# Index scores of a streaming encoder: heads taken two at a time, both PSUM banks claimed, the two 64-row products issued one behind the other

## The chip, the cores and the metric

The kernel runs on one core of one Trainium2 chip. The metric is device time in microseconds (us) of one execution of the program; a lower time is better. Engines are named as the profile names them: PE is TensorE (PEld its weight loads), DVE is VectorE, ACT is ScalarE, POOL is GpSimd, and SP is SyncE, which here only issues DMAs. Each engine takes its own instructions strictly in the order in which they were written for it; an instruction that waits holds up all that stands behind it on that engine.

## The reference

One layer of an encoder is applied to 512 prompt rows and 64 sample rows, 1024 wide, in float32. What matters here is the sparse attention's indexer. Each row has 8 small index queries of 64 numbers and 8 head weights; each key has one index vector of 64 numbers:

```
dots  = einsum('bqhd,bld->bqhl', qi, ki_all) * (IDX_DIM ** -0.5)          # 8 heads, IDX_DIM = 64
score = einsum('bqh,bqhl->bql', wi * (N_IDX_HEADS ** -0.5), relu(dots))   # one number for a row and a key
score = where(admissible, score, NEG_INF)
_, idx = top_k(score, top_k)        # the keys that this row attends to
...                                 # softmax attention over them, 8 heads of 128
y = conv_branch(...)                # depthwise convolution of 31 taps, LayerNorm, swish, projection
mix = (g_att * (o @ w_att_out) + g_conv * y) @ w_o
...                                 # LayerNorm, then a mixture of 16 experts, then LayerNorm
```

The products with the big weights (`w_in`, `w_conv_out`, `w_att_out`, `w_o`) come before, between and after these steps.

## The kernel before

Rows are taken in five tiles: t = 0 to 3 are 128 prompt rows each, t = 4 is the 64 sample rows. A product with a big weight is done in three parts, since weight and input are both split into a rounded high part and the rest (`whi`, `wlo`; `hh`, `hl`). ACT casts `whi` (line 139), DVE subtracts to get `wlo` (line 140), and PE runs three passes for each piece (lines 242 to 244 in `fm_step`, where weights are stationary and 288 tokens stream, the output tile is `acc`; lines 144 to 146 with tokens stationary). `whi` and `wlo` have three buffers, so a cast waits until PE has read an old one.

`select(t)` computes the index scores of a tile and marks the best keys. For each of the 8 heads PE multiplies the head's queries with all keys of the tile's range (line 528): 128 columns of queries are stationary, L keys stream, L is 256, 384 and 512 for t = 1, 2, 3 and 192 for t = 4 (t = 0 needs no selection). The contracted length is only 64. Two heads share a slab of `qiT`: even heads lie in partitions 0 to 63 and odd heads in partitions 64 to 127, and `kiT` holds the keys twice, once in each half. Each float32 product becomes two instructions on PE. The result goes to a PSUM bank of the group `dot`, which has two banks:

```
    def dot(name="dot"):
        return psum.tile([128, 512], F32, name=name, tag="dot", bufs=2)
```

ACT takes it out with a Relu into `rl` (line 530, two buffers), and DVE weighs and adds it to `sc` (lines 532 and 534). DVE then finds the best keys in rounds of a maximum of eight and a replacement (lines 540 and 541) and turns `sc` into a bias. The attention's logits `pl` (line 652) use the same two `dot` banks; DVE reads them in `softmax` (line 639). ACT and PE follow with exponentials, transposes `pp` (line 656) and products `po` (line 660).

Around these steps stand, in program order, the query projections (`tm`, with `stq` taken out by ACT on line 570), the convolution of 8 channel blocks on DVE (line 588), its LayerNorm (lines 612 to 629), 16 gate logits (`gate_logits`, an `fm` product each, its tanh `glg` by ACT on line 709), the split of the convolution's output into `yh` and `yl` (lines 720 and 721), then the products with `w_conv_out` (line 735, inputs `yh`, `yl`) and `w_att_out` (line 741, inputs `oh`, `ol`). The instruction order on each engine is not the program's order: a scheduler with a model of the engines sorts all of it ahead of time, by priority and by when it believes operands to be ready. So the gate logits' and the convolution's `fm` products fill PE between the steps of selection and attention. In the experts' stage the order of PE, DVE and ACT is written by hand, and SP issues the weight loads `ring` (line 1083) behind reads of expert numbers into its registers (line 1308, `TENSOR_LOAD order`).

Of the kernel before, what the change touches and what calls it, by code (L numbers as in the profile page):

```python
# [14 lines left out]
AF = mybir.ActivationFunctionType  # L15
OP = mybir.AluOpType
# [42 lines left out]
def encoder_step(ctx: ExitStack, tc: tile.TileContext, a, o):  # L59
    nc = tc.nc  # L60
    V, S, G, PE, SY = nc.vector, nc.scalar, nc.gpsimd, nc.tensor, nc.sync
# [21 lines left out]
    def trp(name="trp"):  # L83
        return psum.tile([128, 512], F32, name=name, tag="trp", bufs=2)

    def dot(name="dot"):
        return psum.tile([128, 512], F32, name=name, tag="dot", bufs=2)
# [187 lines left out]
    def first_steps(ks):  # L275
        for i in range(3):
            for k in ks:
                for h in range(2):
                    st = fm_step(gps[i], gw3[i], h, k, hh, hl)
        return st  # L280
# [5 lines left out]
    for c in range(4):  # L286
# [4 lines left out]
        st = first_steps([2 * c])  # L291
# [38 lines left out]
    def fm(src, ncols, c0, xh, xl, m=128):  # L330
        with tc.high_priority(offset=400):
            raw = wcols(src, ncols, c0, m)
            ada_next("load")
            with tc.issue_after(hlast):
                w = split(raw, [128, KT, m])
        ps = [acc(), acc()]
        ada_next("product")
        for h in range(2):
            for k in range(KT):
                fm_step(ps, w, h, k, xh, xl, m)  # L340
        return ps
# [90 lines left out]
    qiT = at2[:, 0:2304].rearrange("p (h t) -> p h t", h=4)  # L432
    kiT = at2[:, 2304:3008]
# [18 lines left out]
    def tm(c0, n, kstep):  # L452
        ps = [(acc, acc, acc, dot, fifth)[t](f"tm{t}") for t in range(NT)]
        for k0 in range(0, KT, kstep):
            with tc.high_priority():
                raw = wload(dap(a["w_in"], k0 * 128 * NIN + c0, [[NIN, 128], [128 * NIN, kstep], [1, n]]),
                            [128, kstep, n])
                wh, wl = split(raw, [128, kstep, n])
            order = [(k, t) for k in range(k0, k0 + kstep) for t in range(NT)]
            if k0 + kstep == KT:  # L460
                order = [(k, t) for t in range(NT) for k in range(k0, KT)]
            tokens_product(ps, k0, kstep, hh, hl, hs, wh, wl)
        return ps
# [11 lines left out]
    def rope_heads(x, n, nh, rot, tab):  # L475
        rope(x.rearrange("p (h d) -> p h d", h=nh), rot,
             lambda c0, w: tab[0:n, None, c0:c0 + w].to_broadcast([n, nh, w]))


    def turn(dst, src, t):  # L480
        if t < 4:
            PE.transpose(dst, src, ident)
        else:
            PE.matmul(dst, src, ident2, start=True, stop=True)
# [4 lines left out]
    ps = fm(a["w_in"], NIN, C_KI, hh, hl, 72)  # L489
# [20 lines left out]
    ps = tm(C_QI, 512, 2)  # L510
    for t in range(NT):
        n = TS[t]
        st = misc.tile([128, 512], F32, name="st", tag=("S", "rl")[t % 2], bufs=2)
# [4 lines left out]
            turn(pk[:, 128 * i:128 * i + n], st[:, 128 * i:128 * i + 128], t)  # L518
        S.copy(qiT[:, :, 128 * t:128 * t + n], pk.rearrange("p (h t) -> p h t", h=4)[:, :, 0:n])

    def select(t):
        n, L, k0 = TS[t], (128 * (t + 1), 192)[t == 4], (0, SEQ)[t == 4]
        rounds = (KP, KS)[t == 4] // 8
        sc = misc.tile([128, L], F32, name=f"sc{t}", tag=f"sc{t}", bufs=1)
        for h in range(8):
            pr = slice(64 * (h % 2), 64 * (h % 2) + 64)
            pdt = dot("pdot")
            PE.matmul(pdt[0:n, 0:L], qiT[pr, h // 2, 128 * t:128 * t + n], kiT[pr, k0:k0 + L], start=True, stop=True)  # L528
            rl = misc.tile([128, 512], F32, name="rl", tag="rl", bufs=2)
            S.activation(rl[0:n, 0:L], pdt[0:n, 0:L], AF.Relu, scale=0.125)  # L530
            if h == 0:
                V.tensor_scalar(sc[0:n, 0:L], rl[0:n, 0:L], wis[0:n, t, 0:1], 0.0, op0=OP.mult, op1=OP.add)
            else:
                V.scalar_tensor_tensor(sc[0:n, 0:L], rl[0:n, 0:L], wis[0:n, t, h:h + 1], sc[0:n, 0:L],
                                       op0=OP.mult, op1=OP.add)
        if t < 4:
            V.memset(sc[0:64, L - 64:L], NEG)
        m8 = misc.tile([128, 8], F32, name="m8", tag="m8", bufs=2)
        for r in range(rounds):
            V.max(m8[0:n], sc[0:n, 0:L])  # L540
            V.match_replace(sc[0:n, 0:L], m8[0:n], sc[0:n, 0:L], MARK)
        V.tensor_scalar(sc[0:n, 0:L], sc[0:n, 0:L], MARK, NEG, op0=OP.not_equal, op1=OP.mult)
        return sc

    ps = tm(C_K, 512, 2)
    for t in range(NT):
        n = TS[t]
        st = misc.tile([128, 512], F32, name="stk", tag=("S", "rl")[t % 2], bufs=2)
# [16 lines left out]
    for c in range(2):  # L565
        ps = tm(C_Q + 512 * c, 512, 2)
        for t in range(NT):
            n = TS[t]
            st = misc.tile([128, 512], F32, name="stq", tag=("S", "rl")[t % 2], bufs=2)
            S.copy(st, ps[t])  # L570
            rope_heads(st, 128, 4, 32, rq[:, t, :])
            pk = trp("pq")
            for i in range(4):
                turn(pk[:, 128 * i:128 * i + n], st[:, 128 * i:128 * i + 128], t)
            S.copy(qT[:, 4 * c:4 * c + 4, 128 * t:128 * t + n], pk.rearrange("p (h t) -> p h t", h=4)[:, :, 0:n])
# [26 lines left out]
    bias = {0: bias0}  # L602
# [31 lines left out]
    SCL = HD ** -0.5  # L634

    def softmax(pl, bias, L):
        lg = misc.tile([128, 512], F32, name="lg", tag="lg", bufs=3)
        sm = misc.tile([128, 4], F32, name="sm", tag="sm", bufs=4)
        V.tensor_tensor_reduce(lg[:, 0:L], pl[:, 0:L], bias[:, 0:L], -SCL, 3e38, OP.add, OP.min, sm[:, 0:1])
        S.activation(lg[:, 0:L], lg[:, 0:L], AF.Exp, bias=sm[:, 0:1], scale=-1.0, accum_out=sm[:, 1:2])  # L640
        V.reciprocal(sm[:, 2:3], sm[:, 1:2])
        S.activation(lg[:, 0:L], lg[:, 0:L], AF.Copy, scale=sm[:, 2:3])
        return lg

    def att_prompt(t):
        L = 128 * (t + 1)
        for g in range(2):
            po = fifth("po")
            for hh_ in range(4):
                h = 4 * g + hh_  # L650
                pl = dot("pl")
                PE.matmul(pl[:, 0:L], qT[:, h, 128 * t:128 * t + 128], kT[:, g, 0:L], start=True, stop=True)  # L652
                lg = softmax(pl, bias[t], L)
                pp = trp("pp")
                for kb in range(t + 1):
                    PE.transpose(pp[:, 128 * kb:128 * kb + 128], lg[:, 128 * kb:128 * kb + 128], ident)
                pT = misc.tile([128, 512], F32, name="pT", tag="S", bufs=2)
                S.copy(pT[:, 0:L], pp[:, 0:L])
                for kb in range(t + 1):
                    PE.matmul(po[:, 128 * hh_:128 * hh_ + 128], vtm[:, kb, 128 * g:128 * g + 128],  # L660
                              pT[:, 128 * kb:128 * kb + 128], start=kb == 0, stop=kb == t)
            pov = po.rearrange("p (h t) -> p h t", h=4)
            dst = (slice(None), slice(4 * g, 4 * g + 4), slice(128 * t, 128 * t + 128))
            S.copy(oh[dst], pov)
            V.tensor_tensor(ol[dst], pov, oh[dst], op=OP.subtract)

    def att_sample():
        for g in range(2):
# [21 lines left out]
            V.tensor_tensor(ol[dst], pov, oh[dst], op=OP.subtract)  # L690

    bias[1] = select(1)
    bias[2] = select(2)
    att_prompt(0)
    conv_ln()
    bias[4] = select(4)
    twice = G.dma_start(bias[4][64:128, 0:192], bias[4][0:64, 0:192]).ins
    bias[3] = select(3)
# [150 lines left out]
    ps = [(acc, acc, acc, dot, fifth)[t](f"o{t}") for t in range(NT)]  # L849
# [117 lines left out]
    for t in range(NT):  # L967
        n = TS[t]
# [54 lines left out]
    for j in range(2):  # L1023
        V.tensor_tensor(Ej[:, j], Ej[:, j], bc(w12[:, :, j], 16), op=OP.mult)
        for t in range(NT):
            n = TS[t]
            PE.matmul(pwt[:, 0:16], ohr[0:n, j, t, :].bitcast(F32), Ej[0:n, j, t, :], start=t == 0 and j == 0,
                      stop=t == NT - 1 and j == 1)
# [337 lines left out]
    with tc.manual_schedule(engines={mybir.EngineType.PE, mybir.EngineType.DVE, mybir.EngineType.Activation}):  # L1366
# [15 lines left out]
        for u, x in enumerate(units):  # L1382
            if u == 2:
                for y in units:
                    i = y.es[0] - NFIX
# [126 lines left out]
    for t in range(NT):  # L1512
        n, s = TS[t], int(t == 4)
# [50 lines left out]
```

## Time and profile before

| what | us |
|---|---|
| three timed executions: lowest, median, highest | 869.45, 880.91, 880.99 |
| the profiled execution, its own time | 876.71 |
| its span, first to last instruction | 875.0 |
| PE busy in the span | 791.9 |
| DVE busy | 640.5 |
| ACT busy | 358.6 |
| all 64 instructions of the index products (line 528), first and last start | 278.4 and 394.8 |

The profile is that of one execution. Its span and the execution's own time differ by 1.7 us, which lie ahead of the first and behind the last instruction. The profile gives busy time per engine, the idle time ahead of each group of instructions and what ended it, the instructions in order of time, and the chain of waits: the work that ended last, followed backwards from the end. Matmuls overlap in the pipeline and their ends are modelled, so the distance between two starts says more of their price than the length of one.

### The profile page before, as it was taken

The page shows a single profiled execution, that of the slowest core. Times are in us where ns is not written, and L with a number is a line of the kernel's source. Part 1 is how long each engine was busy: PE and PEld are TensorE (multiplying, and loading weights), DVE is VectorE, ACT ScalarE, POOL GpSimd, SP SyncE. Part 2 cuts the span into 40 slices and gives each one's busy share as a digit, 9 for nine tenths or more (in the row PEclk, how much of TensorE's full clock was granted, in tenths as well). Part 3 has the DMA queues.
Part 4 walks back from the last instruction along what each step waited for, and adds up shares of the span by engine and source line. Part 5 has one row for each costly group of instructions (what it writes and reads, how often), then busy time and mean ns, then how long its engine had stood idle before and what let it go on. Part 6 is the DMA issues. An engine that isn't in the chain of part 4 may idle for free.

```text
span 875.0 us, 13257 instructions
## 1 busy us (share of the span) xinstructions
PE 791.9 (90%) x4827; PEld 640.9 (73%) x4827; DVE 640.5 (73%) x1255; ACT 358.6 (41%) x654; POOL 143.6 (16%) x172
## 2 busy tenths in 40 slices
PE   4899999999999999999999999799947999999920
PEld 3788888887878879879899789788836667645400
DVE  1569999989999889988896425437797697555516
ACT  3243232324344335547743852222433564344205
POOL 2300000310200000000100001020257532322220
PEclk9999999999999999999999999899956999999975
DMA  9997664491423224232443105677597999799525
GB/s 289 342 352 254 204 201 126 120 246 56 148 75 89 83 75 115 89 100 62 135 127 106 54 1 194 224 214 260 116 273 242 346 348 316 200 335 386 149 46 201
DMA packets 108866, 159.70 MB, mean 183 GB/s; under 512 B 9715, under 2 KB 67211, under 8 KB 108801
## 3 DMA queue, kind: packets, MB, share of 16 engines
q1 hardware_dynamic: 94464, 120.38, 42.1%
q0 software_dynamic: 12736, 34.26, 15.3%
q10 hardware_dynamic: 1600, 4.22, 1.3%
q8 instruction: 38, 0.62, 0.3%
q14 instruction: 28, 0.22, 0.1%
HBM read 143.65 MB, written 26.13 MB: 194 GB/s over the span
## 4 chain that ended last, share of the span: by engine, by line
PE 58%; DVE 7%; DMA 7%; issue 2%; ACT 2%; POOL 1%; POOLq 0%; SPq 0%; DVEq 0%; ACTq 0%
PE acc L242 7%; PE acc L244 7%; PE acc L243 7%; PE pd L1175 4%; PE pdot L528 3%; PE pg L1145 2%; DMA wraw<-in_w_att_out_dram 2%; PE tm L144 2%; PE tm L146 2%; PE tm L145 2%; PE pl L652 2%; PE po L660 2%; PE pg L144 2%; DMA z_scr<-yo,idt 2%; PE pg L146 2%
## 5 line engine op out<-in xcount | busy, mean ns | idle before, releaser
L588 DVE SCALAR_TENSOR_TENSOR y<-ue,dwT,y 128x604 f32<-128x604 f32 (+17 forms) x232 | 183.2, 828 | 1.9 <-ACT y L586 1.5
L242 PE MATMUL acc<-hh,wlo 128*128 128x288 f32 (+1 forms) x504 | 152.7, 304 | 1.6 <-DVE wlo L140 1.6
L243 PE MATMUL acc<-hh,whi 128*128 128x288 f32 (+1 forms) x504 | 150.4, 299 | 0.0
L244 PE MATMUL acc<-hl,whi 128*128 128x288 f32 (+1 forms) x504 | 149.3, 300 | 0.0
L139 ACT CAST whi<-wraw 128x1024 fp32r<-128x1024 f32 (+1 forms) x72 | 75.0, 1043 | 172.7 <-PE acc L244 85.5
L140 DVE TENSOR_TENSOR wlo<-wraw,whi 128x1024 fp32r<-128x1024 f32 (+1 forms) x72 | 87.4, 1214 | 52.6 <-ACT whi L139 52.3
L242 PEld LDWEIGHTS acc<-hh,wlo 128*128 128x128 f32 (+1 forms) x504 | 94.2, 187 | 17.5 <-issue 8.8
L243 PEld LDWEIGHTS acc<-hh,whi 128*128 128x128 f32 (+1 forms) x504 | 94.2, 187 | 5.2 <-issue 5.1
L244 PEld LDWEIGHTS acc<-hl,whi 128*128 128x128 f32 (+1 forms) x504 | 93.7, 187 | 5.5 <-issue 5.2
L144 PE MATMUL tm<-wlo,hh 128*128 128x512 f32 x128 | 50.5, 397 | 0.4 <-DVE wlo L140 0.4
L145 PE MATMUL tm<-whi,hh 128*128 128x512 f32 x128 | 50.4, 393 | 0.0
L146 PE MATMUL tm<-whi,hl 128*128 128x512 f32 x128 | 49.8, 392 | 0.0
L140 DVE TENSOR_TENSOR wlo<-ring,whi 128x1024 fp32r<-128x1024 f32 x30 | 36.3, 1222 | 13.2 <-ACT whi L139 13.0
L1175 PE MATMUL pd<-ring,hT 128*128 128x512 f32 x96 | 44.5, 607 | 1.0 <-ACT hT L1159 1.0
L242 PE MATMUL acc<-oh,wlo 128*128 128x288 f32 x128 | 39.4, 308 | 5.6 <-DVE gt L744 5.1
L139 ACT CAST whi<-ring 128x1024 fp32r<-128x1024 f32 x30 | 31.3, 1049 | 29.0 <-PE pg L146 25.4
L244 PE MATMUL acc<-yl,whi 128*128 128x288 f32 x128 | 39.3, 310 | 0.6 <-DVE yl L721 0.5
L1190 POOL DMA_INDIRECT z_scr<-yo,idt x16 | 28.3, 1769 | 68.6 <-DMA z_scr<-yo,idt 29.8
L244 PE MATMUL acc<-ol,whi 128*128 128x288 f32 x128 | 39.2, 309 | 0.0
L243 PE MATMUL acc<-oh,whi 128*128 128x288 f32 x128 | 39.1, 306 | 0.0
L243 PE MATMUL acc<-yh,whi 128*128 128x288 f32 x128 | 38.3, 301 | 0.0
L242 PE MATMUL acc<-yh,wlo 128*128 128x288 f32 x128 | 37.9, 297 | 0.0
(474 smaller groups left out, 1769.0 us busy)
## 6 DMA issues: line engine op xcount, KB each, us to landing
ring<-in_w_gate_up_dram SPq DMA_DIRECT2D x62, 512.0 KB, 8.5
wraw<-in_w_in_dram SPq DMA_DIRECT2D x48, 512.0 KB, 4.9
wada<-in_w_ada_dram SPq DMA_DIRECT2D x32, 512.0 KB, 6.0
ring<-in_w_down_dram SPq DMA_DIRECT2D x32, 512.0 KB, 10.6
wada<-in_w_ada_dram SPq DMA_DIRECT2D x32, 256.0 KB, 6.2
gates_scr<-glg POOLq DMA_DIRECT2D x16, 288.0 KB, 2.6
gt<-gates_scr POOLq DMA_DIRECT2D x16, 288.0 KB, 3.1
wraw<-in_w_conv_out_dram SPq DMA_DIRECT2D x8, 512.0 KB, 4.0
```

The lines of the kernel that those rows point to most:

```text
L139: split_copy[0] = S.copy(hi, raw).ins
L140: V.tensor_tensor(lo, raw, hi, op=OP.subtract)
L144: PE.matmul(out, lh, rl, start=start, stop=False)
L145: PE.matmul(out, lh, rh, start=False, stop=False)
L146: PE.matmul(out, ll, rh, start=False, stop=stop)
L242: PE.matmul(ps[h][0:m, 0:288], wl[:, k, :], xh[:, k, sl], start=k == 0, stop=False)
L243: PE.matmul(ps[h][0:m, 0:288], wh[:, k, :], xh[:, k, sl], start=False, stop=False)
L244: return PE.matmul(ps[h][0:m, 0:288], wh[:, k, :], xl[:, k, sl], start=False, stop=k == KT - 1).ins
L528: PE.matmul(pdt[0:n, 0:L], qiT[pr, h // 2, 128 * t:128 * t + n], kiT[pr, k0:k0 + L], start=True, stop=True)
L588: V.scalar_tensor_tensor(y[:, 30 - i:EXT], ue[:, 0:EXT - 30 + i], dwT[:, j, i:i + 1], y[:, 30 - i:EXT], op0=OP.mult, op1=OP.add)
L1175: PE.matmul(pd_[c], hT[:, k, :], dns[0][k][:, cs], start=k == 0, stop=k == 1)
L1190: sc = G.indirect_dma_start(out=z_d, out_offset=bass.IndirectOffsetOnAxis(ap=idx[0:128 // len(ids)], axis=0), in_=y[half], in_offset=None, ...
```

## The change

The loop over the 8 heads takes them in pairs. At an even head both `dot` banks are claimed and both products are issued, the even head's from partitions 0 to 63 and the odd head's from partitions 64 to 127. The second is bound to stand straight behind the first in PE's order (`issue_after`). The first of the two also waits for the last reader of both banks: `bank_read` remembers the newest instruction that took a bank out, which is the odd head's Relu of the pair before, a softmax's first DVE step, or, for the first pair of all, the copy of the last query projection's fourth tile (`t == 3`, whose `ps` is a `dot` bank too). The Relus and the additions to `sc` stay one for each head.

```diff
+    bank_read = [None]
     def select(t):
...
         for h in range(8):
-            pr = slice(64 * (h % 2), 64 * (h % 2) + 64)
-            pdt = dot("pdot")
-            PE.matmul(pdt[0:n, 0:L], qiT[pr, h // 2, 128 * t:128 * t + n], kiT[pr, k0:k0 + L], start=True, stop=True)
+            if h % 2 == 0:
+                pds = [dot("pdot"), dot("pdot")]
+                mm = []
+                for i in range(2):
+                    pr = slice(64 * i, 64 * i + 64)
+                    with tc.issue_after(mm[0]) if i else nullcontext():
+                        mm.append(PE.matmul(pds[i][0:n, 0:L], qiT[pr, h // 2, 128 * t:128 * t + n], kiT[pr, k0:k0 + L],
+                                            start=True, stop=True).ins)
+                tc.add_manual_dep(mm[0], bank_read[0].name,
+                                  mybir.DependencyInfo(mybir.DependencyClass.Sync, mybir.DependencyReason.DATA),
+                                  reason="both of the banks are free")
             rl = misc.tile([128, 512], F32, name="rl", tag="rl", bufs=2)
-            S.activation(rl[0:n, 0:L], pdt[0:n, 0:L], AF.Relu, scale=0.125)
+            bank_read[0] = S.activation(rl[0:n, 0:L], pds[h % 2][0:n, 0:L], AF.Relu, scale=0.125).ins
...
-            S.copy(st, ps[t])
+            read = S.copy(st, ps[t]).ins
+            bank_read[0] = read if t == 3 else bank_read[0]
...
-        V.tensor_tensor_reduce(lg[:, 0:L], pl[:, 0:L], bias[:, 0:L], -SCL, 3e38, OP.add, OP.min, sm[:, 0:1])
+        bank_read[0] = V.tensor_tensor_reduce(lg[:, 0:L], pl[:, 0:L], bias[:, 0:L], -SCL, 3e38, OP.add, OP.min,
+                                              sm[:, 0:1]).ins
```

Since the scheduler sorts anew, the change also moves other instructions. Three places follow; `x2` means two alike in a row, and line numbers of the kernel after the change are larger (528 is 535, 530 is 541, 709 is 722, 1083 is 1096, 1308 is 1321).

PE, in `select(2)` (384 keys), between `fm` products of a gate logit; before, two heads with four `fm` passes between them:

```order
L244 MATMUL acc<-hl,whi 128x288
L528 MATMUL pdot<-at_1572 128x384
L242 MATMUL acc<-hh,wlo 128x288
L243 MATMUL acc<-hh,whi 128x288
L244 MATMUL acc<-hl,whi 128x288
L242 MATMUL acc<-hh,wlo 128x288
L528 MATMUL pdot<-at_1572 128x384
L243 MATMUL acc<-hh,whi 128x288
```

The same tile after the change, its third pair:

```order
L242 MATMUL acc<-hh,wlo 128x288
L243 MATMUL acc<-hh,whi 128x288
L244 MATMUL acc<-hl,whi 128x288
L535 MATMUL pdot<-at_1572 128x384 x2
L242 MATMUL acc<-hh,wlo 128x288
```

The two products now stand together, and the four `fm` passes that lay between two heads lie elsewhere; there are 16 such places where there were 30.

ACT in the same tile before (`rl` is a head's Relu, `glg` a gate's tanh, which waits for PE's `fm` product, `whi` a cast of weights):

```order
L709 ACTIVATE glg<-acc 128x288
L530 ACTIVATE rl<-pdot 128x384
L709 ACTIVATE glg<-acc 128x288
L530 ACTIVATE rl<-pdot 128x384 x2
L139 CAST whi<-wraw 128x1024
```

ACT after:

```order
L722 ACTIVATE glg<-acc 128x288
L541 ACTIVATE rl<-pdot 128x384
L722 ACTIVATE glg<-acc 128x288
L541 ACTIVATE rl<-pdot 128x384
L139 CAST whi<-wraw 128x1024
L722 ACTIVATE glg<-acc 128x288
L541 ACTIVATE rl<-pdot 128x384 x2
```

ACT's order hardly moves: in this pair a tanh stands between the even head's Relu and the odd head's, which is the one that the next pair on PE waits for.

SP in the experts' stage before (a load of expert weights between reads of expert numbers):

```order
L1083 DMA ring<-in_w_gate_up_dram 128x2x512
L1308 TENSOR_LOAD order
L1308 ISA x2
L1083 ISA
L1083 DMA ring<-in_w_gate_up_dram 128x2x512
L1308 TENSOR_LOAD order
```

SP after:

```order
L1096 DMA ring<-in_w_gate_up_dram 128x2x512
L1321 TENSOR_LOAD order
L1321 ISA x2
L1321 TENSOR_LOAD order
L1321 ISA x2
L1096 ISA
L1096 DMA ring<-in_w_gate_up_dram 128x2x512
```

One load has moved behind one more read of a number; the rest of SP's order and all of POOL's are as before.

## Rows read from the trace of the kernel before

**Rows 1.** Page, part 1: busy us (share of the span), instructions.

```profile
PE 791.9 (90%) x4827; PEld 640.9 (73%) x4827; DVE 640.5 (73%) x1255; ACT 358.6 (41%) x654; POOL 143.6 (16%) x172
```

**Rows 2.** Stretches: PE, PEld, DVE, ACT, POOL busy; clock; DMA share; GB/s.

```profile
278.35:422.10 143.75, 143.61 (x925) 122.57 (x924) 127.25 (x283) 75.24 (x155) 8.67 (x16) 1.00 0.32 92
422.10:484.00 61.90, 61.34 (x451) 59.28 (x450) 51.73 (x129) 27.65 (x68) 5.58 (x10) 1.00 0.39 113
430.00:470.00 40.00, 40.00 (x304) 39.46 (x303) 37.95 (x95) 15.82 (x39) 3.97 (x7) 1.00 0.44 125
484.00:530.00 46.00, 45.25 (x310) 38.43 (x309) 16.60 (x54) 29.94 (x69) 0.54 (x1) 1.00 0.07 19
```

**Rows 3.** Chain of waits: start us, us, what.

```profile
423.47 0.67 DVE yl L721
...
424.62 0.67 DVE yl L721
...
425.33 0.40 PE acc L244
...
535.37 18.57 DMA wraw<-in_w_att_out_dram
```

**Rows 4.** Groups in 278.35 to 422.10: busy, mean ns, idle before and its releasers.

```profile
L140 DVE TENSOR_TENSOR wlo<-wraw,whi 128x1024 fp32r<-128x1024 f32 x16 | 19.5, 1220 | 11.9 <-ACT whi L139 11.9
L139 ACT CAST whi<-wraw 128x1024 fp32r<-128x1024 f32 x16 | 16.8, 1047 | 26.7 <-PE acc L244 26.3 <-PE tm L160 0.3
...
L530 ACT ACTIVATE rl<-pdot 128x256 f32<-128x256 f32 (+3 forms) x32 | 14.2, 448 | 12.7 <-PE pdot L528 12.2 <-DVE sc L541 0.5
L709 ACT ACTIVATE glg<-acc 128x288 f32<-128x288 f32 x31 | 12.6, 407 | 16.3 <-PE acc L244 16.3
```

**Rows 5.** PE in order of time: one product each of 256, 384, 192, 512 keys.

```profile
293.28 0.29 PE L243 MATMUL acc<-hh,whi 128*128 128x288 f32 x1
293.51 0.70 PE L528 MATMUL pdot<-at 64*128 64x256 f32 x2
...
294.37 0.30 PE L242 MATMUL acc<-hh,wlo 128*128 128x288 f32 x1
...
307.34 0.29 PE L242 MATMUL acc<-hh,wlo 128*128 128x288 f32 x1
307.56 0.91 PE L528 MATMUL pdot<-at 64*128 64x384 f32 x2
...
308.64 0.30 PE L244 MATMUL acc<-hl,whi 128*128 128x288 f32 x1
...
308.90 0.29 PE L243 MATMUL acc<-hh,whi 128*128 128x288 f32 x1
...
366.23 0.29 PE L243 MATMUL acc<-hh,whi 128*128 128x288 f32 x1
366.45 0.54 PE L528 MATMUL pdot<-at 64*64 64x192 f32 x2
...
367.15 0.30 PE L242 MATMUL acc<-hh,wlo 128*128 128x288 f32 x1
...
370.33 0.29 PE L243 MATMUL acc<-hh,whi 128*128 128x288 f32 x1
370.56 1.12 PE L528 MATMUL pdot<-at 64*128 64x512 f32 x2
...
371.85 0.29 PE L242 MATMUL acc<-hh,wlo 128*128 128x288 f32 x1
```

**Rows 6.** PE in order of time: two heads of the sample tile that stand together.

```profile
357.57 0.54 PE L528 MATMUL pdot<-at 64*64 64x192 f32 x4
```

**Rows 7.** Line 528 in 357.62 to 357.70 and 357.8 to 358.0: ns min/median/max, starts.

```profile
L528 PE MATMUL pdot<-at x2: 373/373/373, 357.6 to 357.6; 64*64 64x192 f32 x2
...
L528 PE MATMUL pdot<-at x4: 322/348/373, 357.6 to 357.8; 64*64 64x192 f32 x4
```

**Rows 8.** SP's issues in order of time, experts' stage: start us, us.

```profile
672.36 12.79 SPq L1083 DMA_DIRECT2D ring<-in_w_gate_up_dram  x10
```

## The prediction

> **What bounds the kernel now.** The page's first part comes first: PE is busy for 90% of the span, DVE for 73%, ACT for 41% [rows 1]. An average over stages says little, so the second view is the stretches. The index products run from 278.4 to 394.8 us, and in 278.35 to 422.10 PE is busy for 143.61 of 143.75 us at full granted clock, while DVE is busy for 127.25 and ACT for 75.24 [rows 2]. PE therefore sets the pace there. DVE has 143.75 - 127.25 = 16.5 us of idle time, and the groups of that stretch say what ends it: 11.9 us are `wlo` waiting for ACT's cast of `whi`, and that cast in turn sat idle for 26.3 us until PE had finished with an old `whi` [rows 4]. DVE's idle time hangs on PE, so a faster PE gives it back to DVE, but there are only 16.5 us of it.
>
> The chain of waits shows where the two engines meet. Between 423.47 and 425.3 us it runs through DVE's `yl`, and at 425.33 it goes back to PE's `acc` [rows 3]: the products with `w_conv_out` need `yh` and `yl`, which DVE makes at the end of the convolution's LayerNorm. So by about 422 us DVE has also only just got there. Behind that point PE is the bound alone: in 422.10 to 484.00 it is busy for 61.34 of 61.90 us and DVE for 51.73, in 484.00 to 530.00 for 45.25 of 46.00 us against DVE's 16.60 [rows 2]. What is won by 422 us stays won until 530 us. The 18.57 us wait for a load of `w_att_out` at 535.37 [rows 3] could hide a gain if its time were fixed from the start of the program; the loads around it are issued when buffers come free and when earlier products are merged, so I let it move along with the rest.
>
> **What a product costs PE.** A price is read from starts: from the start of the `fm` pass ahead to the start of the second pass behind, less two plain steps, which take 308.90 - 308.64 = 0.26 us [rows 5]. For 256 keys that is 294.37 - 293.28 - 0.26 = 0.83 us, for 384 keys 308.64 - 307.34 - 0.26 = 1.04, for 512 keys 371.85 - 370.33 - 0.26 = 1.26, for the sample tile's 192 keys 367.15 - 366.23 - 0.26 = 0.66 [rows 5]. From 256 to 512 keys the price grows by 0.43, so about 0.83 - 0.43 = 0.40 us of each is a fixed price of the change from `fm` passes to a 64-row product and back. In all there are 8 products of each kind, but in the sample tile four of the eight already stand two by two, so it has six places: 8 x (0.83 + 1.04 + 1.26) + 6 x 0.66 = 25.0 + 4.0 = 29.0 us of PE's time.
>
> **What a pair costs.** The trace of before has two pairs, both in the sample tile. The one at 357.57 holds four instructions in 0.54 us; a single product at 366.45 holds two in the same 0.54 us [rows 5, 6]. Looked at closely, two of the four are on record as starting at 357.6 and running 373 ns, and the other two as starting by 357.8 [rows 7]: the two heads' first halves run at the same time, then their second halves. So products from partitions 0 to 63 and 64 to 127 do run side by side, and a pair costs one. That is shown for 64 stationary columns. With 128 columns (t = 1 to 3) no pair is on record; the bounds are the price of one product, by the nearest row, and that of two with only one fixed price saved, 0.40 us. I take the first, since the two products differ in nothing but rows and bank, as in the row.
>
> With that, PE's time falls to 4 x (0.83 + 1.04 + 1.26) + 4 x 0.66 = 15.2 us: **13.8 us less**. At the other bound it falls by 12 x 0.40 = 4.8 us, and by nothing if two products bring their fixed price each.
>
> The Trainium skill bears on this in TensorE: Matmul & The Clock Gate, section Measured speedup vs the span model: four row tiles of 32 rows gave 3.07 times the speed, not 4. As an estimate from that page, a pack would cost 1.3 singles, and the twelve pairs of t = 1 to 3 would save 25.0 - 12.5 x 1.3 = 8.7 us instead of 12.5. The pair in the trace shows no such surcharge.
>
> **How much of it reaches the end.** ACT and DVE have as much to do as before: 32 Relus of 448 ns on ACT [rows 4] and the same additions on DVE. If PE were 13.8 us faster to 422 us, DVE would have to be busy for 127.25 of 130.0 us, 98%. The densest long stretch on record is 430 to 470 us, with 37.95 of 40 us, 94.9% [rows 2]. I take that as what DVE can reach among its waits for ACT: 127.25 / 0.949 = 134.1 us, so **9.7 us** of the 143.75 go, and at the end of the stretch PE waits some 4 us for `yl` instead of next to nothing. Before, DVE was the one with room; after, DVE would be the bound from about 280 to 425 us.
>
> **The added wait.** The first product of a pair waits until the odd head's Relu of the pair before has read its bank. Behind it on PE stand the `fm` passes. The Relus come at once: ACT sat idle for 12.2 us in this stretch until a product was there, and a Relu takes 448 ns [rows 4]. In the new order at least 16 `fm` passes lie between two pairs of a prompt tile, at 0.13 us each 2.1 us or more, with four transposes beside them in the shortest gap; two Relus and a tanh between them take 2 x 0.448 + 0.407 = 1.30 us [rows 4]. I cost the wait at nothing while that cover lasts; uncovered it is at most 1.30 us a pair.
>
> **What else moves.** PE's, DVE's and ACT's orders keep their shape: the same steps in the same sequence, with the `fm` passes dealt out differently. On SP one load of expert weights goes behind one more read of a number. Ten such loads with the reads between them took 12.79 us [rows 8], so it can be later by 1.3 us at most; I take nothing, as the loads behind it are issued as before. The end of attention without cover from `fm` passes (484 to 530 us) has the same steps in both orders.
>
> **Sum.** 876.71 - 9.7 = **867.0 us**, against the profiled execution. The median of the three timed executions lies 4.2 us above that one and their lowest 7.3 below, so the same saving from the median would read 871.2.
>
> **Rivals.** (1) *DVE follows all the way.* Its 16.5 us of idle time are more than 13.8, and nearly all hangs on PE. Then the whole saving stands: 862.9 us. Against it speaks that DVE would run at 98%.
>
> (2) *The pairs with 128 columns do not run side by side*, or run so only in part. Then PE saves 0 to 4.8 us plus 1.3 of the sample tile: 870.6 to 875.4 us, 873 in the middle. For it: no such pair is on record; against it, the two in the sample tile.
>
> (3) *The readers of the banks hold PE up, and the kernel gets slower.* Before, PE could start a head while ACT still read the other bank; now no product starts until both are read, and a tanh that waits for PE, or a Relu that waits for a free `rl`, can stand in between on ACT. If each of the 16 pairs waits 1.30 us in full, that is 20.8 us against 13.8 saved: 883.7 us. It turns from a gain into a loss at 13.8 / 16 = 0.86 us a pair. Against it: ACT waits for PE in this stretch, not PE for ACT. The Trainium skill, in TensorEngine Tiling (Array Packing), section PSUM Bottleneck, warns of just this: tiling speeds up the products, not the emptying of PSUM, which may become the bottleneck. No run so far shows it at work here; ACT is busy for 75.24 of 143.75 us in the stretch.
>
> **Chances and range.** The forecast (DVE takes over after some 10 us) gets 0.50, rival 1 gets 0.18, rival 2 gets 0.18, rival 3 gets 0.09; 0.05 is left for a sorting of the other stages that I have not seen the effect of. Executions of the same kernel lay between 869.45 and 880.99, 7 us below and 4 above the profiled one, so each of these has such a spread around it. From rival 1 with part of that spread below it (857) to the upper end of rival 2 with the spread above it (880), no more than 2 in 10 is left out: 857 to 880 us. A difference of 2% is about what a measurement of this kernel can tell from no change, and 2% is 17.5 us. The largest saving here is 13.8 us, so faster by over 2% needs rival 1 and luck with the spread, 0.13; slower by over 2% needs rival 3 at over twice its price, 0.04; within 2%, 0.83.
>
> **What would show it.** In the profile after: the four instructions of a pair with 128 columns should take the time of two now (0.70, 0.91, 1.12 us), and line 535 should hold PE for some 15 us in place of 29. The stretch from the first index product to the first product on `yh` should shrink by about 10 us with DVE at 95%, DVE's wait of `wlo` for `whi` should fall from 11.9 to a few us, and PE should show a wait for `yl` of a few us. If PE shows waits for `rl` ahead of pairs, rival 3 is at work; if a pair takes 1.2 us at 256 keys, rival 2. The forecast is wrong if the gain appears by 425 us and is gone at the end, or if DVE's busy share in the stretch stays near 89% while PE waits.

## The result, and the profile after

| | before | after |
|---|---|---|
| median of the timed executions, us | 880.95 (869.45 to 882.26, 4 runs) | 865.55 (862.35 to 867.09, 4 runs) |
| the profiled execution, its own time | 876.71 | 862.35 |
| its span | 875.0 | 860.7 |

The ratio after to before is 0.9871, with a 95% interval of 0.9822 to 0.9921: the kernel became faster by 0.8 to 1.8%. The ratio goes by fast executions alone and is not the quotient of the two medians, which is 0.983. Two further series beside the kernel before, below, gave 0.9813 and 0.9810.

The page of the kernel after, its first part, beside [rows 1]:

```profile
PE 774.9 (90%) x4827; PEld 633.9 (74%) x4827; DVE 639.8 (74%) x1255; ACT 358.3 (42%) x654; POOL 137.9 (16%) x172
```

PE has lost 17.0 us of busy time with the same number of instructions (14.8 and 13.2 us in the profiles of the two repeats below); DVE and ACT have lost under 1 us. The first stretch of [rows 2] in the kernel after, from the first index product to 1.2 us ahead of the first `yl` (408.5 us; before, the stretch ended at it, 422.1); the columns are the busy times of PE, PEld, DVE, ACT and POOL, the clock, the DMA share and GB/s:

```profile
281.01:407.25 126.24, 126.20 (x898) 114.67 (x897) 122.78 (x273) 72.72 (x153) 8.13 (x15) 1.00 0.34 101
```

The stretch is 126.24 us long instead of 143.75, but it also begins later, at 281.0 instead of 278.4, and ends a little earlier in the program; at one and the same point, the first `yl`, the kernel after is 13.6 us ahead. PE is as full as before; DVE, which was busy for 127.25 of 143.75 us (89%), is now busy for 122.78 of 126.24 (97.3%). The groups of that stretch say where DVE found the room (busy, mean ns, idle time before and its releasers):

```profile
L140 DVE TENSOR_TENSOR wlo<-wraw,whi 128x1024 fp32r<-128x1024 f32 x16 | 19.5, 1219 | 0.1
L139 ACT CAST whi<-wraw 128x1024 fp32r<-128x1024 f32 x15 | 15.7, 1050 | 15.1 <-PE acc L244 15.1
...
L541 ACT ACTIVATE rl<-pdot 128x256 f32<-128x256 f32 (+3 forms) x32 | 13.4, 447 | 15.1 <-PE pdot L535 12.8 <-DVE sc L545 2.2
L535 PE MATMUL pdot<-at 64*128 64x256 f32 (+3 forms) x64 | 13.2, 488 | 0.0
L722 ACT ACTIVATE glg<-acc 128x288 f32<-128x288 f32 x31 | 12.6, 408 | 7.6 <-PE acc L244 7.3
```

DVE's wait of `wlo` for `whi`, 11.9 us before [rows 4], is down to 0.1: PE gives back the old weights sooner, so ACT casts sooner. PE in order of time, a pair of 256 and one of 512 keys, beside the single products of [rows 5]:

```profile
298.20 0.29 PE L244 MATMUL acc<-hl,whi 128*128 128x288 f32 x1
298.42 0.70 PE L535 MATMUL pdot<-at 64*128 64x256 f32 x4
299.05 0.40 PE L242 MATMUL acc<-hh,wlo 128*128 128x288 f32 x1
...
377.57 1.13 PE L535 MATMUL pdot<-at 64*128 64x512 f32 x4
378.63 0.40 PE L244 MATMUL acc<-hl,whi 128*128 128x288 f32 x1
```

Four instructions take 0.70 us where two took 0.70, and 1.13 where two took 1.12. Line 535 in 298.40 to 298.50 and in 298.70 to 299.0 (ns min/median/max, then the starts) shows how:

```profile
L535 PE MATMUL pdot<-at x2: 480/480/480, 298.4 to 298.4; 64*128 64x256 f32 x2
...
L535 PE MATMUL pdot<-at x4: 376/428/480, 298.4 to 298.7; 64*128 64x256 f32 x4
```

The first halves of both heads start together at 298.4, their second halves together at 298.7, as in the sample tile's pair before [rows 7], now with 128 columns. From a place's start to the next instruction's start, summed over all places, the index products took 22.95 us before and 12.04 after.

The chain of waits of the kernel after, where it goes from DVE to PE, beside [rows 3] (start us, us, what):

```profile
409.77 0.68 DVE yl L734
410.45 0.04 issue
410.49 0.40 PE acc L244
```

The chain goes over at 410.49 us instead of 425.33, but at the second of the eight blocks of `yl` instead of the third, so these two times are not those of one instruction. The first product on `yh` is: it starts at 407.57 us instead of 420.94, 13.4 us forward, with 2714 PE instructions ahead of it in both kernels. PE shows no wait for `yl` there (0.5 us before). The last attention product (`po`) starts at 511.1 us instead of 525.7, 14.6 forward; the span is shorter by 14.3.

### The profile page after: what moved, and what is told of

The parts are those of the page before. It is cut to its first block, busy times and chain, and to the rows that moved or that the text cites. A ratio compares the mean times of both kernels' runs of the same rounds, so it can differ in the third digit from the quotient of the medians.

```text
span 860.7 us, 13259 instructions
## 1 busy us (share of the span) xinstructions
PE 774.9 (90%) x4827; PEld 633.9 (74%) x4827; DVE 639.8 (74%) x1255; ACT 358.3 (42%) x654; POOL 137.9 (16%) x172
## 3 DMA queue, kind: packets, MB, share of 16 engines
q0 software_dynamic: 12736, 34.26, 15.4%
## 4 chain that ended last, share of the span: by engine, by line
PE 56%; DVE 10%; DMA 4%; ACT 3%; issue 2%; another core or an unknown queue 1%; POOL 0%; POOLq 0%; SPq 0%; DVEq 0%; ACTq 0%
PE acc L242 6%; PE acc L244 6%; PE acc L243 6%; PE pd L1188 5%; PE pg L144 3%; PE pg L146 3%; PE pg L1158 3%; PE pg L145 2%; PE tm L144 2%; PE po L673 2%; PE tm L146 2%; PE tm L145 2%; DMA z_scr<-yo,idt 2%; PE pxt L1140 2%; PE o L144 2%
## 5 line engine op out<-in xcount | busy, mean ns | idle before, releaser
L1203 POOL DMA_INDIRECT z_scr<-yo,idt x16 | 26.5, 1656 | 73.2 <-DMA z_scr<-yo,idt 29.7
```

The costliest lines, as they stand in the source:

```text
L1203: sc = G.indirect_dma_start(out=z_d, out_offset=bass.IndirectOffsetOnAxis(ap=idx[0:128 // len(ids)], axis=0), in_=y[half], in_offset=None, ...
```

## The experiments

They are read in two ways: by the median against the kernel before on the same chip, and by the profile, where the start of the last `po` shows what the stages up to the end of attention took. The kernel before has it at 525.7 us, the changed kernel at 511.1. This start repeats well: three profiles of the changed kernel put it at 511.1, 511.7 and 511.1 us. The time from there to the end does not: it lay between 339.4 and 349.6 us over the twelve profiles, with the same work on DVE and ACT, and the median of the kernel before lay between 870.97 and 880.95 us in its four series. So medians are compared within one series only.

**The changed kernel again**, twice, as the yardstick in the first and in the third series.

> The changed kernel once more, as the yardstick for the kernels beside it. Both theories expect what the first result showed: about 865 us, 11 to 15 us below the kernel before, and in the profile about 15.2 us from start to start for the 16 pairs.

> The changed kernel once more beside the kernel that follows; both theories: a ratio of 0.980 to 0.988 to the kernel before, the last attention product at about 511 us.

Measured: 862.51 us against 878.73, ratio 0.9813 (0.9771 to 0.9854), and 857.98 against 872.51, ratio 0.9810 (0.9764 to 0.9856). The last `po` started at 511.7 and 511.1 us. The gain repeats; the first result lies at the small end of it.

**The pair in the same rows.** The odd head's product takes its operands from partitions 0 to 63 too:

```diff
-                    pr = slice(64 * i, 64 * i + 64)
+                    pr = slice(0, 64)
```

> The odd head's product takes the even head's queries and the lower copy of the keys (partitions 0 to 63), so the two products of a pair share rows; the odd heads' scores are those of the even heads. PE's and DVE's orders are those of the changed kernel, word for word. Theory A (the gain comes from the two products running at the same time): a pair now costs two products less at most one fixed price, 1.3 to 1.7 us at 256 keys and 2.1 to 2.5 at 512, PE loses 9 to 13.8 us of its saving, and the time is 874 to 879 us. Theory B (the gain comes from the new order or from fewer changes between kinds of passes): a pair still costs two without a fixed price, and the time stays near 865 to 870 us.

Measured: 868.8 us against 878.73, ratio 0.9885 (0.9845 to 0.9926). PE in order of time, a pair of 256 and one of 512 keys:

```profile
299.32 0.29 PE L244 MATMUL acc<-hl,whi 128*128 128x288 f32 x1
299.55 1.13 PE L535 MATMUL pdot<-at 64*128 64x256 f32 x4
300.60 0.40 PE L242 MATMUL acc<-hh,wlo 128*128 128x288 f32 x1
...
384.22 1.98 PE L535 MATMUL pdot<-at 64*128 64x512 f32 x4
386.13 0.40 PE L244 MATMUL acc<-hl,whi 128*128 128x288 f32 x1
```

From start to the next start a pair takes 1.05 and 1.91 us instead of 0.63 and 1.06; over all 16 pairs 20.97 instead of 12.04 us. Read as the prediction reads a price, with the passes around it, these pairs cost 1.26 and 2.11 us, the low ends of theory A's ranges. With the same order on PE, DVE and ACT, the last `po` starts at 520.3 us: 9.2 us later than with pairs across the rows (8.6 later than in the repeat beside it), 5.4 us earlier than in the kernel before. So the saving up to there has two parts: **9.2 us from running side by side, 5.4 us from the new order with pairs standing together**. Of the second part 4.2 us are there by the first product on `yh` (416.76 us against 420.94): the fixed price of going from `fm` passes to a 64-row product and back, paid at 16 places instead of 30, about 0.30 us for each place less. The other 1.2 us came behind that product, where PE's waits in 270 to 530 us fell from 1.2 to 0.3 us. Theory A had allowed for the fixed price (0.40 us at each of 12 pairs, 4.8 us). The median misses theory A's 874 to 879 all the same: it gives back 6.3 us of 16.2, the profile 9.2 of 14.6. The profiles place that difference behind the last `po`, where this kernel took 344.3 us and the repeat beside it 347.6, which is within the spread named above; what causes the spread stays open. Theory B, which had no gain from running side by side, falls.

**Without the wait for both banks.** The five lines with `add_manual_dep` left out:

```diff
-                tc.add_manual_dep(mm[0], bank_read[0].name,
-                                  ...
-                                  reason="both of the banks are free")
```

> Without the added dependence on the last reader of both banks; each product still waits for the reader of its own bank. Theory A: the added wait costs nothing, so the time is that of the changed kernel within 2 us, unless the second product of a pair is late for its bank and the halves no longer start together. Rival (the wait holds PE up somewhere that the profile does not name): 2 to 6 us faster than the changed kernel.

Measured: 875.91 us against 878.73, ratio 0.9991 (0.9947 to 1.0035), the last `po` at 525.9 us: the whole gain is gone. Theory A had named the case (a second product that is late for its bank) as an exception, but neither theory had expected it. The order of PE, DVE and ACT is then that of the kernel before, instruction by instruction. PE at the place of the second head:

```profile
293.64 0.70 PE L535 MATMUL pdot<-at 64*128 64x256 f32 x2
```

The products stand alone again. So `issue_after` does not bind the second product to stand straight behind the first, as the section on the change has it: it only keeps it from coming earlier. The likely reason for the gap is that the even head's bank is free one Relu earlier than the odd head's, so that the scheduler issues the first product and fills in `fm` passes until the second bank is free; this is read from the code and was not tried by itself. What the run shows is that **the added wait is what makes a pair**. As this kernel is in effect the kernel before, its two medians also show what a measurement is worth: 2.8 us apart.

**One product for two heads.** PE's price of a pair with only one product in it; both Relus read it:

```diff
-                for i in range(2):
+                for i in range(1):
...
-            ... S.activation(rl[0:n, 0:L], pds[h % 2][0:n, 0:L], AF.Relu, scale=0.125).ins
+            ... S.activation(rl[0:n, 0:L], pds[0][0:n, 0:L], AF.Relu, scale=0.125).ins
```

> Only the even head's product is issued, and both Relus of a pair read it; the odd heads' scores are those of the even heads. PE has half the index products and each place holds two instructions. Theory A (a pair costs what one product costs): the time of the changed kernel within 2 us. Theory B (pairs run side by side only in part): 3 to 9 us faster than the changed kernel.

Measured: 869.22 us against 878.73, ratio 0.987 (0.9834 to 0.9905), the last `po` at 519.4 us. Theory B falls, as this kernel is not faster than the pairs; but it is 6.7 us slower, which theory A had not expected either. The products do cost the same, 11.94 us from start to next start against 12.04. What PE waited for in 270 to 530 us (us in total, times, longest):

```profile
PE acc L242 <- ACT yh L733: 6.1, 2, 5.7
PE acc L242 <- ACT oh L677: 0.9, 1, 0.9
PE pp L669 <- ACT lg L655: 0.4, 1, 0.4
```

These are 7.4 us instead of the pairs' 0.3, out of the 8.3 us by which the last `po` is later. PE stood 6.1 us of them where it takes up the products on `yh`. Its order is another one, since the scheduler sorted anew, and in it the index products come later: the groups in 281 to 412.5 us show DVE waiting for `rl` for 5.5 us and ACT for the products for 18.0:

```profile
L545 DVE SCALAR_TENSOR_TENSOR sc<-rl,wis,sc 128x256 f32<-128x256 f32 (+3 forms) x28 | 15.6, 558 | 5.5 <-ACT rl L541 5.5
L541 ACT ACTIVATE rl<-pdot 128x256 f32<-128x256 f32 (+3 forms) x32 | 13.2, 446 | 18.0 <-PE pdot L535 18.0
```

With the pairs these were 1.6 and 12.8 us. So the new theory: with PE's saving DVE has hardly any idle time left, and whatever DVE loses in waits up to `yl` appears at the last `po`. The next runs test it by taking work from PE, from DVE, and from both.

**Four places on PE instead of 16** (one product for each row tile, read by all 8 Relus):

```diff
-            if h % 2 == 0:
+            if h == 0:
...
-                for i in range(2):
+                for i in range(1):
```

> On the changed kernel: one index product for each row tile, read by all 8 Relus, so 4 places on PE instead of 16; the scores of heads 1 to 7 are those of head 0. PE loses another 3 x (0.83 + 1.04 + 1.26 + 0.66) = 11.4 us. Theory A (with the pairs DVE has run out of room: 122.78 of 126.24 us busy): no more than 3.5 us faster than the pairs, and PE shows a wait for yh or yl of 6 us or more. Theory B (PE is still the only bound and DVE gives way): 8 to 11 us faster than the pairs, about 852 us.

**Fewer taps**, on the changed kernel and on the kernel before:

```diff
-        for i in range(28, -1, -1):
+        for i in range(28, -1 if j < 6 else 6, -1):
```

> On the changed kernel: 14 of the convolution's multiply-adds left out (7 taps of the last two channel blocks), 14 x 0.826 = 11.6 us less for DVE in the stretch of the index products. Theory A (PE at 99.9% is as much a bound as DVE): the time of the pairs within 2 us. Rival (DVE alone is the bound after the change): 5 to 11 us faster.

> The same 14 multiply-adds left out of the kernel before. Both theories: PE alone was the bound there, so the time of the kernel before within 3 us. If it is 5 us or more faster, DVE held the kernel before up too, and the reading of its trace was wrong.

**Both cuts.**

> Both cuts on the changed kernel: one index product for each row tile and the 14 multiply-adds left out. Theory A: with room on both engines the 11.4 us come out, 8 to 11 us faster than the pairs, although neither cut alone gives over 3.5. Theory B: no faster than the cut of products alone.

All four stood beside one series of the kernel before, with a median of 870.97 us. The pairs had no run in this series, so what the theories say against the pairs' time is read from the last `po`:

| kernel | median, us | ratio (95%) | last `po`, us |
|---|---|---|---|
| four places on PE | 859.79 | 0.9874 (0.9843 to 0.9906) | 513.5 |
| fewer taps, changed kernel | 856.69 | 0.9847 (0.9814 to 0.9880) | 511.2 |
| fewer taps, kernel before | 869.39 | 0.9977 (0.9953 to 1.0002) | 524.1 |
| both cuts | 854.39 | 0.9818 (0.9792 to 0.9845) | 506.9 |

What PE waited for in 270 to 530 us with four places:

```profile
PE acc L242 <- ACT yh L733: 9.0, 1, 9.0
PE acc L244 <- DVE yl L734: 2.1, 1, 2.1
```

The index products took 2.98 us from start to next start instead of 12.04, and PE stood for 9.0 + 2.1 = 11.1 us instead: a further saving of PE's time turns into waiting, and none of it reaches the end of attention; the last `po` even came 2.4 us later than with the pairs. Theory B falls. Taking the 14 multiply-adds from DVE alone (its busy time fell by 10.5 and 10.6 us) moves the last `po` by 0.1 us on the changed kernel and by 1.6 on the kernel before: PE is a bound in both. Both cuts together bring 4.2 us up to the last `po`, where neither alone brought any, and 6.6 against the cut of products alone, so theory B falls here too; but it is not the 8 to 11 of theory A. PE's 11.1 us of waiting for `yh` and `yl` came down to 1.6 when DVE had less to do, which speaks for DVE's work as what had made them late, although each of these orders was sorted anew; new waits came up, for `gt` (2.4 us), `glg` (1.8) and `oh` (0.9). The ratios show no clear gain over the pairs for any of the three cuts of the changed kernel: the pairs had 0.9810 to 0.9871 in their series.

**One product for two heads, with fewer taps.**

> One product for two heads, as in the earlier run, and the 14 multiply-adds of the last two channel blocks left out as well. There PE paid for the index products what it pays with the pairs, but stood 6.1 us for yh. Theory A (DVE was late there, since the sorted order left it waiting for products, and every us that DVE saves up to that point comes out): PE's wait for yh goes below 2 us and the last attention product ends at 511 to 514 us instead of 519.4, 5 to 8 us faster. Rival (something else in that order costs PE the time): the last attention product stays at 517 to 520 us.

Measured: 864.35 us against 872.51, ratio 0.9888 (0.9847 to 0.993). The wait for `yh` fell from 6.1 to 1.1 us, as theory A says, but the last `po` came at 515.8 us, between theory A's 511 to 514 and the rival's 517 to 520: 3.6 earlier than without the cut and 4.7 later than with the pairs. The ratio shows nothing of this, 0.9888 beside 0.987. So 3.6 of that kernel's 8.3 us went with DVE's work. Most of the other 4.7 are waits again, 4.0 us of them in 270 to 530 us instead of 0.3, two thirds of them inside attention:

```profile
PE pp L669 <- ACT lg L655: 2.0, 1, 2.0
PE acc L242 <- ACT yh L733: 1.1, 1, 1.1
PE pl L665 <- DVE sm L651: 0.6, 2, 0.4
PE acc L242 <- ACT oh L677: 0.3, 1, 0.3
```

Which part of the new sorting makes these waits was not tried.

## Why the prediction was right, and where it was not

- **What bounds the kernel before**: right. PE alone set the pace, and 14 multiply-adds less on DVE moved the last `po` by only 1.6 us there.
- **A pair costs one product**: right, and to the hundredth. The row of the sample tile, 64 columns wide, held for 128 columns: 0.63 us at 256 keys and 1.06 at 512. The price of 1.3 singles that was estimated from the Trainium skill (TensorE: Matmul & The Clock Gate, Measured speedup vs the span model, which measured four tiles of 32 rows) did not appear with two tiles of 64: at 256 keys a pair took 0.633 us and a single product 0.626.
- **PE's saving of 13.8 us**: right. It was 13.4 us at the first product on `yh` and 14.6 at the last `po`. By the prediction's way of reading a price, the places cost 28.6 us before (it had 29.0) and 15.4 after (15.2). The same-rows run splits the 13.4 into 9.2 for running side by side and 4.2 for fewer places; the sum had 13.8 - 4.8 = 9.0 and 4.8 in it.
- **DVE takes over after 9.7 us: this is the step that failed, by its size.** The 94.9% was no limit: DVE was busy for 97.3% of the stretch, 13.4 us came out instead of 9.7, and PE did not wait for `yl`, where some 4 us had been forecast. DVE followed all the way, which was rival 1 with a chance of 0.18. The reading behind the 94.9% was wrong too, since 430 to 470 us is not the densest long stretch of the trace before. In 200 to 270 us DVE was busy for 98.8% and PE for 99.4% (columns as in [rows 2]):

```profile
200.00:270.00 70.00, 69.56 (x329) 55.82 (x328) 69.14 (x140) 25.95 (x47) 5.46 (x10) 1.00 0.34 100
```

Most of DVE's work there is the convolution, which waits little, so this does not prove that the stretch of the index products could be filled as far; it takes away the ground for 94.9%, and with it the objection to rival 1.
- **The time that was forecast**: near the result in part by luck. Against the profiled execution rival 1 gave 862.9 us, and the profiled execution after took 862.35; but that is the fastest of the four. That the median of 865.55 lies nearer to the forecast of 867.0 is due to the base: it lies 15.4 us under a median that was itself 4.2 above the profiled execution.
- **DVE as the next bound**: right, only later than forecast. The next cut of PE's time, estimated at 11.4 us, came back as 11.1 us of waiting.
- **The added wait at nothing**: right in its price, as PE shows no wait for `rl`. Not foreseen was its use: without it there are no pairs.
- **What moves besides**: the last `po` moved by 14.6 and the span by 14.3 us. That these agree is luck, as two differences of some 6 us cancel: from the last `po` to the last `mh` (ACT's rounding of the merged rows, which the product with `w_o` takes in) the profile after took 45.3 us instead of 51.5, and from there to the end 304.3 instead of 297.8. The changed kernel's third profile took 52.5 and 295.7, so neither is a price of the new order as far as these runs show, the load that went behind one more read on SP included. The new sorting was taken as of no account because the sequence of steps kept its shape; the run with one product for two heads, where PE paid the same for the index products, shows that such a sorting can cost 7 us.
- **Rivals 2 and 3** did not come about. The warning of the Trainium skill's TensorEngine Tiling (Array Packing), PSUM Bottleneck, that emptying PSUM may become the bottleneck, did not come true here: ACT, which empties the banks, was busy for 72.72 of 126.24 us. What stopped a further saving on PE, as far as the two cuts show, was DVE's work.

## What to carry to other kernels

In this kernel two float32 products of 64 contracted rows, from the lower and the upper half of the partitions and into two banks, cost PE as much as one if they stand next to each other (0.63 us at 256 keys); look in the trace for a place where they already do, and read the price there. That they stand next to each other had to be forced by what they wait for, since this scheduler's rule that one comes after the other let `fm` passes in between. Before counting on a second saving of the same kind, add up the idle time that the next engine has left in that stretch: it was 16.5 us before, 3.5 after, and the next cut came back as waiting. Before taking a busy share as an engine's limit, look through the whole trace for a stretch that goes above it.

## What the runs showed of the hardware that was not expected

The load of `w_att_out` on which the chain of waits stands behind attention took 9.78 us in one profiled execution of the changed kernel and 19.70 in another:

```profile
519.25 9.78 DMA wraw<-in_w_att_out_dram
```

```profile
520.77 19.70 DMA wraw<-in_w_att_out_dram
```

By the last cast of `mh` the second was 7.2 us behind (563.6 against 556.4 us), and yet its span was shorter, 859.3 against 860.7 us. Between the last `mh` and the end the first took 304.3 us and the second 295.7. In these two, what was lost at the load was made up behind it. It is not always made up in full: in the order of the kernel before, the load took 18.57 us in one profile [rows 3] and 14.81 in the other (the run without the wait for both banks), the last `mh` came 5.9 us sooner behind the last `po` in the second, and 3.4 of these were left at the end. So the length of this wait in one profile is no fixed price of a kernel, and how much of a shorter wait would show at the end stays open: these executions did not all run on one chip, and no run tried the load by itself.
